# A three-engine scan put into the order of the source: a Trainium2 trunk of a gating MLP, an RWKV-7 layer and two ConvFFNs

## The chip, the core and the metric

The kernel runs on one core of one Trainium2 chip. A core has TensorE (PE, matrix products into PSUM), VectorE (DVE), ScalarE (ACT) and GpSimd (POOL), each with an instruction queue of its own, and SyncE (SP), which here only starts transfers. Each queue is a program of its own, and semaphores order the engines among each other. The metric is the device time of one execution in microseconds; lower is better. The kernel before has a median of 1274.5 us over three runs (1272.83 to 1276.07).

## The reference

One sequence of 512 positions with 1024 features goes through two residual layers. Layer 0 is a gating MLP (SGU) and a ConvFFN, layer 1 an RWKV-7 mixer and a ConvFFN; each sub-layer has an RMSNorm ahead of it. The part of the RWKV mixer that the change touches is the scan, for 16 heads of 64:

```python
def step(state, inp):
    r_t, w_t, k_t, v_t, a_t, b_t = inp
    sa = jnp.einsum('bhvk,bhk->bhv', state, a_t)
    state = (state * w_t[:, :, None, :]
             + sa[..., None] * b_t[:, :, None, :]
             + v_t[..., None] * k_t[:, :, None, :])
    y_t = jnp.einsum('bhvk,bhk->bhv', state, r_t)
    return state, y_t
```

and what follows it: a group norm of `y` per head, a bonus term, a gate `g = sigmoid(xg @ g1) @ g2` with `xg` a mix of the normalized input and its shifted copy, and the output projection `(y * g) @ w_o`.

## The kernel before, in words

**Tiling.** Activations lie transposed, as eight tiles of 128 features by 512 positions. Every dense weight product is done in three float32r products (`mm3`, lines 317 to 319: high part by high, high by low, low by high), each 128 rows by 128 columns of the array with 512 columns streamed. One such triple is a step of `dense_steps`.

**The chunked scan.** The 512 positions are cut into 8 chunks of 64 (`NCH`), and the 16 heads into two groups `g` of eight, four tiles `i` by two halves `hd` of the partitions. Within a chunk the recurrence becomes matrix products. `pairs` builds the operands of each chunk (line 935 and 949: products 64 rows deep and 128 columns wide) and sends them to DRAM; `invert(g)` inverts the 64 by 64 triangular matrices of a group. Its part for 32 by 32 blocks is a ladder on VectorE, 31 pairs of a product (line 1011) and a sum (line 1012), behind it two transposes (1017, 1018), and then 32 by 32 products on TensorE (1030, 1033) whose results ScalarE copies (1038, 1043, 1045). The group 1 ladder stands at the border of the pairs and the scan.

**One chunk of the scan** (`scan`) is this chain. Eight products `us` (line 1194, 128 rows by 64 columns) need the state `vu`; VectorE copies them to `wt` (1196). Eight products with the inverse `ti` (1207, 64 by 64) need `wt`; VectorE copies one half of their result back to `vu` (1208), ScalarE the other (1209). Eight products with `bt` (1216) need both halves; VectorE adds `s0` to them (1219, two instructions) and so writes the `vu` of the next chunk. `s0` comes from GpSimd (1203). Off this chain lie eight products `e` (1198) and eight more (1221) that make the output `y`, copied by ScalarE (1224). After each second chunk `finish` normalizes 128 positions of `y`: square on ScalarE (1237), sum on VectorE (1240), a power on GpSimd (370), a product on VectorE (1243), four transposes on TensorE (1247) and four multiply-adds on VectorE (1250).

**What fills TensorE between them.** `fill` is one long generator: the projections of `r`, `k` and `v` with their followers (`value`: transposes at 829 with copies at 834, a product of 512 columns at 844, an addition at 846, an activation at 847; line 842 makes the weights of 844), then `gates`, then the output projections (`project`). In `gates`, `gate_mix(k)` prepares one of eight operands: ScalarE scales (1054), VectorE combines (1055), ScalarE rounds to the high part (236), VectorE subtracts to get the low part (237). It cannot emit the gates of a group before all of that group's `y` is normalized.

**What sets the order.** `weave` steps the scan and puts steps of `fill` behind marked TensorE instructions at given rates. Between the remaining choices a scheduler decides: it orders each engine's queue by priority and by when it reckons an instruction to be ready. So in the scan a ready dense product may be queued ahead of a chain product that the scheduler expects later.

## Time and profile before

| | |
|---|---|
| median of three runs | 1274.5 us (1272.83 to 1276.07) |
| the profiled execution's own time | 1274.33 us |
| its span | 1272.5 us |
| TensorE matmuls busy | 1254.8 us, 7591 instructions |
| VectorE busy | 856.5 us |
| ScalarE busy | 629.6 us |
| first instruction at which the two programs' TensorE orders differ | 710.47 us |
| first product of the first chunk (line 1194) | 737.85 us |
| first product of group 1's first chunk | 803.77 us |
| end of the common stretch: from 874.22 us on TensorE's order is the same again | 874.22 us |

The trace numbers lines by the kernel before. One 32-bit product of the program shows as two matmul records, so that a set of eight shows as x16. Rows of a timeline give start and length in us; a matmul's length is modelled and overlaps its successor, so what a product costs TensorE is read from start to start. Rows of groups give the count, the busy sum in us and the mean of one in ns.

### The profile page before, as it was taken

How to read it: one execution, taken by the hardware profiler on the slowest of the kernel's cores; microseconds unless marked ns; L12 is line 12 of the kernel's file. 1: busy time of each engine (PE TensorE's matmuls, PEld its weight loads, DVE VectorE, ACT ScalarE, POOL GpSimd, SP SyncE). 2: the span in 40 equal slices, each digit the busy share in tenths (PEclk: the TensorE clock that was granted, in tenths of full speed). 3: DMA queues.
4: the chain of work that ended last, by engine and by line, in shares of the span. 5: the costliest groups of instructions: out<-in, count | busy, mean ns of one | idle time of the engine just before them, and what ended most of it. 6: DMA issues, size and time to landing. Idle time of an engine off the chain costs nothing.

```text
span 1272.5 us, 19534 instructions
## 1 busy us (share of the span) xinstructions
PE 1254.8 (99%) x7591; PEld 1014.3 (80%) x7591; DVE 856.5 (67%) x1403; ACT 629.6 (49%) x1082; POOL 98.0 (8%) x119
## 2 busy tenths in 40 slices
PE   9999999999999999999999999999999999999997
PEld 6878888888888888887777776677888888888886
DVE  6466568888886444675789887665677777772233
ACT  5534446555555333475686647423544444443232
POOL 4100200000000000000000022222100000000002
PEclk9999999999999999999999999999999999999999
DMA  7332357887556775335878698763233332233332
GB/s 251 108 99 83 123 173 239 244 255 240 198 169 209 216 231 161 105 106 182 220 203 226 202 245 206 203 181 133 83 99 100 100 99 91 94 94 106 93 91 79
DMA packets 115452, 201.65 MB, mean 158 GB/s; under 512 B 21600, under 2 KB 53600, under 8 KB 115360
## 3 DMA queue, kind: packets, MB, share of 16 engines
q10 hardware_dynamic: 39104, 112.87, 29.4%
q1 hardware_dynamic: 76256, 87.54, 23.1%
q8 instruction: 59, 0.97, 0.3%
q14 instruction: 33, 0.27, 0.1%
HBM read 152.93 MB, written 47.45 MB: 157 GB/s over the span
## 4 chain that ended last, share of the span: by engine, by line
PE 90%; DVE 4%; issue 1%; DMA 0%; POOL 0%; ACT 0%; DVEq 0%; ACTq 0%; POOLq 0%
PE mm L317 10%; PE mm L319 9%; PE mm L318 9%; PE aux L317 6%; PE aux L319 6%; PE aux L318 6%; PE e L318 6%; PE e L317 6%; PE e L319 6%; PE us L319 5%; PE us L318 5%; PE us L317 5%; PE aux L935 1%; PE aux L949 1%; PE us L1194 1%; PE e L1221 1%
## 5 line engine op out<-in xcount | busy, mean ns | idle before, releaser
L236 ACT CAST w<-w 128x512 fp32r<-128x512 f32 x340 | 206.8, 611 | 364.6 <-PE aux L319 91.8
L237 DVE TENSOR_TENSOR w<-w,w 128x512 fp32r<-128x512 f32 x340 | 232.1, 685 | 185.2 <-ACT w L236 184.7
L317 PE MATMUL mm<-mxh,w 128*128 128x512 f32 (+1 forms) x416 | 170.5, 410 | 0.0
L318 PE MATMUL mm<-mxl,w 128*128 128x512 f32 (+1 forms) x416 | 164.6, 396 | 0.0
L319 PE MATMUL mm<-mxh,w 128*128 128x512 f32 (+1 forms) x416 | 164.3, 395 | 0.0
L344 POOL TENSOR_TENSOR ss<-ss,sq 128x512 f32<-128x512 f32 x30 | 40.6, 1353 | 771.1 <-issue 592.9
L317 PEld LDWEIGHTS mm<-mxh,w 128*128 128x128 f32 (+1 forms) x416 | 77.6, 187 | 20.0 <-issue 3.3
L319 PEld LDWEIGHTS mm<-mxh,w 128*128 128x128 f32 (+1 forms) x416 | 77.8, 187 | 17.4 <-issue 0.7
L318 PEld LDWEIGHTS mm<-mxl,w 128*128 128x128 f32 (+1 forms) x416 | 77.9, 187 | 16.1 <-issue 1.3
L542 ACT ACTIVATE cv<-z,par 128x512 f32<-128x512 f32 x88 | 71.7, 817 | 28.1 <-DVE z L540 23.1
L317 PE MATMUL aux<-mxh,w 128*128 128x512 f32 x216 | 84.5, 391 | 0.0
L319 PE MATMUL aux<-mxh,w 128*128 128x512 f32 x216 | 84.2, 390 | 0.3 <-DVE w L237 0.3
L317 PE MATMUL us<-mxh,w 128*128 128x512 f32 x216 | 84.5, 391 | 0.0
L318 PE MATMUL aux<-mxl,w 128*128 128x512 f32 x216 | 84.1, 389 | 0.0
L318 PE MATMUL us<-mxl,w 128*128 128x512 f32 x216 | 84.1, 389 | 0.0
L319 PE MATMUL us<-mxh,w 128*128 128x512 f32 x216 | 84.0, 389 | 0.0
L317 PE MATMUL e<-mxh,w 128*128 128x512 f32 x208 | 81.4, 391 | 0.1
L318 PE MATMUL e<-mxl,w 128*128 128x512 f32 x208 | 81.1, 390 | 0.1
L319 PE MATMUL e<-mxh,w 128*128 128x512 f32 x208 | 80.9, 389 | 0.0
L543 DVE SCALAR_TENSOR_TENSOR cv<-z,par,cv 128x512 f32<-128x512 f32 x88 | 66.1, 752 | 20.0 <-ACT cv L542 20.0
L544 DVE SCALAR_TENSOR_TENSOR cv<-z,par,cv 128x512 f32<-128x512 f32 x88 | 66.0, 752 | 2.9
L319 PEld LDWEIGHTS aux<-mxh,w 128*128 128x128 f32 x216 | 40.5, 187 | 9.2 <-DVE w L237 0.8
(1088 smaller groups left out, 2599.0 us busy)
## 6 DMA issues: line engine op xcount, KB each, us to landing
w<-in_wup ACTq DMA_DIRECT2D x88, 512.0 KB, 3.7
w<-in_wdn ACTq DMA_DIRECT2D x32, 512.0 KB, 3.6
st<-std SPq DMA_DIRECT2D x30, 320.0 KB, 6.1
w<-wkd ACTq DMA_DIRECT2D x16, 512.0 KB, 4.8
w<-wvd ACTq DMA_DIRECT2D x16, 512.0 KB, 5.6
w<-wod ACTq DMA_DIRECT2D x16, 512.0 KB, 4.3
w<-in_wdn ACTq DMA_DIRECT2D x16, 384.0 KB, 3.3
w<-in_wsu ACTq DMA_DIRECT2D x8, 512.0 KB, 3.8
```

The source lines that it names most:

```text
L236: nc.scalar.copy(hi[r, :n], src)
L237: (lo_eng or nc.vector).tensor_tensor(lo[r, :n], src, hi[r, :n].bitcast(F32), ALU.subtract)
L317: mm(acc, wh, xh, start=first, stop=False)
L318: mm(acc, wh, xl, start=False, stop=False)
L319: mm(acc, wl, xh, start=False, stop=last)
L344: nc.gpsimd.tensor_tensor(self.ss, self.ss, self.sq, ALU.add)
L542: nc.scalar.activation(c, z[:, 2:], AF.Identity, scale=cw(2, i), bias=self.p("conv_b", l * 44 + i))
L543: nc.vector.scalar_tensor_tensor(c, z[:, 1:T + 1], cw(1, i), c, ALU.mult, ALU.add)
L544: nc.vector.scalar_tensor_tensor(c, z[:, 0:T], cw(0, i), c, ALU.mult, ALU.add)
L935: nc.tensor.matmul(qs[hd][:, c - ch.start, :], bk[H[hd], c, C * hd:C * hd + P], ar[H[hd], c, :], start=True, stop=True)
L949: nc.tensor.matmul(qs[hd][:, c, :], bk[H[hd], c, C * hd:C * hd + P], dg[H[hd], c, :], start=True, stop=True)
L1194: nc.tensor.matmul(us[H[hd], 0, i, :], ar(i, hd, 0), vu[:, hd, i, :], start=True, stop=True)
```

## The change

One function `recurrence` takes the place of the two woven scans. It walks both groups in one loop inside a block in which TensorE, VectorE and ScalarE keep the order in which the source emits instructions. Within a chunk:

- The products 1207 of a chunk stand directly behind the eight output products (1221 before, 1189 now) of the chunk ahead of it, which need the same 64 by 64 mode; the output products of a chunk are so put off by one chunk (`pend`).
- Dense work comes in two blocks, behind the products with `ti` and behind those with `bt` (`pump`), each of two steps of `fill` as long as `fill` has dense work.
- The copies of the chain (1208, 1209) are emitted first; output copies, `finish` (in `slot`s), group 1's inversion (`side`) and `fill` come behind them. `finish` goes at most one step per slot.
- `for _ in range(AHEAD)` lets eight steps of group 1's inversion be emitted for one of group 0's, ahead of the scan. The ladder's instructions stand in the program ahead of the block, and the scheduler places them.
- Weight loads of the scan stretch go by SP's queue, no longer by ScalarE's (`self.wq`).
- The gate's second weight part is padded with zeros from 32 to 128 columns, so that its products use the whole array.
- The last `value` takes a bank of `aux`, and the two first mixes and the gate weights are fetched at other steps.

Lines move: 1194, 1196, 1198, 1207, 1208, 1209, 1216, 1219, 1221, 1224 become 1242, 1244, 1246, 1257, 1258, 1259, 1268, 1271, 1189, 1193; 1011, 1012, 1017, 1018, 1030, 1038, 1043 become 1020, 1021, 1026, 1028, 1040, 1048, 1053; 317 to 319 become 325 to 327; 829, 834, 842, 844, 846, 847 become 838, 843, 851, 853, 855, 856; 236 and 237 become 240 and 241, 255 to 257 become 259 to 261; 1054 and 1055 become 1064 and 1065.

```diff
@@ -32,6 +32,9 @@
 
 RATES = ((1.9, 2), (1.9, 6, 2.2), (0.66, 2, 1.15), (0.72, 2), (2, 2), (1.2, 6, 2.2))
 LEAD = 1
+AHEAD, SUBST, PRODUCTS, PUMP = 8, 5, (0, 0, 0, 0, 0, 2, 3, 3), (1.3, 1.3)
+MID = (1.3, 1.3)
+MIDDLE, END = 1, 2
 WB = 4
 FIRST0, WAIT, STEPS = 1, 1, (2, 2, 2, 2, 2)
 NKEY = 3
...
@@ -302,7 +306,10 @@
         t = [self.wp.tile([P, 1024], F32, tag="w32", bufs=2, name=self.uid("w32")) for _ in range(2)]
         for i in range(2):
             self.wq.dma_start(t[i], self.gd[:, i, 0:1024])
-        return (1024, [tuple(x.bitcast(F32R) for x in t)]), (512, [self.pair(self.gd[:, :, 1024:], 256)])
+        w = self.pair(self.gd[:, :, 1024:], 256)
+        for x in w:
+            self.nc.gpsimd.memset(x[:, 256:384].bitcast(F32), 0.0)
+        return (1024, [tuple(x.bitcast(F32R) for x in t)]), (512, [w])
 
     @staticmethod
     def wcols(w, c, n, rows=slice(None)):
...
@@ -314,6 +321,7 @@
 
         mm = self.nc.tensor.matmul
         (wh, wl), (xh, xl) = w, x
+        self.work += 3 * (acc.shape[-1] + 32) / 2400
         mm(acc, wh, xh, start=first, stop=False)
         mm(acc, wh, xl, start=False, stop=False)
         mm(acc, wl, xh, start=False, stop=last)
...
@@ -840,7 +849,7 @@
                 yield
             wb = ip.tile([P, P], F32, tag="wb", bufs=1, name=self.uid("wb"))
             S.activation(wb, self.c("bones", P), AF.Copy, scale=self.p("r_k", m))
-            q = self.acc("mm")
+            q = self.acc("aux" if m == KT - 1 else "mm")
             nc.tensor.matmul(q, wb, rt[g][:, i, :], start=True, stop=True)
             b = rt[g][:, i, :]
             V.tensor_tensor(b, q, v, ALU.mult)
...
@@ -1163,14 +1173,56 @@
                 nc.sync.dma_start(bt, btd[c][:, ps])
             chunks[g, c] = st, bt, vu
 
-        left, two = [], []
-
-        def scan(g, late=iter(())):
-
-            ih = [(i, hd) for i in range(4) for hd in range(2)]
+        two, pend, lates = [], [], []
+
+        def heads():
+            return [(i, hd) for i in range(4) for hd in range(2)]
+
+        def outputs(copy=True):
+
+            if not pend:
+                return
+            g, c, st, vu, e, y = pend[0]
+            if copy is not None:
+                for i, hd in heads():
+                    o = RW * (1 - hd)
+                    nc.tensor.matmul(e[H[hd], 0, i, :], st[i][H[hd], o:o + C], vu[H[hd], hd, i, :],
+                                     start=False, stop=True, skip_group_check=True)
+            if copy is not False:
+                for hd in range(2):
+                    S.copy(y[H[c % 2], :, hd, :], e[H[hd], 0])
+                if c % 2 == 1:
+                    lates.append([finish(g, c // 2, y), MIDDLE])
+                pend.pop()
+
+        def slot(place):
+
+            for late in list(lates):
+                if late[1] != place:
+                    continue
+                with ExitStack() as ctx:
+                    for eng in (mybir.EngineType.PE, mybir.EngineType.DVE):
+                        ctx.enter_context(tc.issue_after(self.last(eng)))
+                    more = next(late[0], None)
+                if more is None:
+                    lates.remove(late)
+                else:
+                    late[1] = more
+
+        def pump(us):
+
+            self.owed += us
+            while self.owed > 0:
+                before = self.work
+                if next(fill, self) is self:
+                    return
+                self.owed -= max(self.work - before, 0.1)
+
+        def recurrence(side):
+
+            ih = heads()
             y = None
-
-            for c in range(NCH):
+            for g, c in itertools.product(range(2), range(NCH)):
                 last = c == NCH - 1
                 if (g, c) not in chunks:
                     load(g, c)
...
@@ -1201,33 +1249,36 @@
                     s0 = tile_([P, 4, C], "wt", 4)
                     for hd in range(2):
                         G.tensor_tensor(s0[H[hd]], vu[H[hd], hd], bc(gc[H[hd], 4 * g:4 * g + 4, c], C), ALU.mult)
-                self.step(late)
-                yield
+                if g == 1 and c == 0:
+                    for _ in side:
+                        pass
+                outputs(False)
                 for i, hd in ih:
                     nc.tensor.matmul(us[H[hd], 1, i, :], ti[g][H[hd], i, c, :], wt[H[hd], i, :], start=True, stop=True)
                 V.tensor_copy(vu[h0, 0], us[h0, 1])
                 S.copy(vu[h1, 1], us[h1, 1])
-                self.step(late)
-                if g == 1 and c == 0:
-                    self.step(late)
-                yield
+                outputs(None)
+                pend.append((g, c, st, vu, e, y))
+                slot(MIDDLE)
+                if g == 0 and c < SUBST:
+                    self.step(side)
+                pump(MID[g])
                 if not last:
                     for i, hd in ih:
                         nc.tensor.matmul(us[H[hd], 0, i, :], bt[:, i, hd, :], vu[:, hd, i, :], start=True, stop=True)
                     nvu = chunks[g, c + 1][2]
                     for hd in range(2):
                         V.tensor_tensor(nvu[H[hd], hd], us[H[hd], 0], s0[H[hd]], ALU.add)
-                for i, hd in ih:
-                    nc.tensor.matmul(e[H[hd], 0, i, :], pt(i, hd), vu[H[hd], hd, i, :],
-                                     start=False, stop=True, skip_group_check=True)
-                for hd in range(2):
-                    S.copy(y[H[c % 2], :, hd, :], e[H[hd], 0])
-                self.step(late)
-                yield
-                if c % 2 == 1:
-                    yield from late
-                    late = finish(g, c // 2, y)
-            left.append(late)
+                slot(END)
+                if g == 0:
+                    for _ in range(1 if c < SUBST else PRODUCTS[c]):
+                        self.step(side)
+                pump(PUMP[g])
+            outputs()
+            while lates:
+                pump(PUMP[g])
+                slot(MIDDLE)
+                slot(END)
 
         def finish(g, b, y):
 
...
@@ -1235,13 +1286,13 @@
             ts = slice(b * P, (b + 1) * P)
             sq = tile_([P, 2 * 4, C], "ysq", 2)
             S.activation(sq, y3, AF.Square)
-            yield
+            yield END
             ss, rs = tmp("gs", 2, 8), tmp("gr", 2, 8)
             V.tensor_reduce(ss, sq, AX.X, ALU.add)
             self.rsqrt(ep, rs, ss, 1.0 / C, GN_EPS)
-            yield
+            yield MIDDLE
             V.tensor_tensor(y3, y3, bc(rs, C), ALU.mult)
-            yield
+            yield END
             q = self.acc("aux")
             for i in range(4):
                 nc.tensor.transpose(q[:, i * P:(i + 1) * P], y[:, i].rearrange("p h f -> p (h f)"), self.c("ident", P))
...
@@ -1308,18 +1358,19 @@
         ahead = invert(1)
         for _ in inv:
             next(fill)
-            self.step(ahead, (mybir.EngineType.PE,))
+            for _ in range(AHEAD):
+                self.step(ahead, (mybir.EngineType.PE,))
         ctx.close()
         ep = ctx.enter_context(tc.tile_pool(name="scan", bufs=1))
         inv = ahead
         r.sg = [ep.tile([P, T], F32R, name=f"sg{i}") for i in range(3)]
         for _ in range(LEAD):
             next(fill, None)
-        self.weave(scan(0), inv, fill, *RATES[2], ktiles=STEPS[2])
-        for _ in inv:
-            pass
-        self.weave(scan(1, left.pop()), None, fill, *RATES[3], ktiles=STEPS[3])
-        self.weave(left.pop(), None, fill, *RATES[4], ktiles=STEPS[4])
+        self.ktiles, self.work, self.owed = 1, 0.0, 0.0
+        self.wq = nc.sync
+        with tc.manual_schedule(engines={mybir.EngineType.PE, mybir.EngineType.DVE, mybir.EngineType.Activation}):
+            recurrence(inv)
+        self.wq = nc.scalar
         for _ in fill:
             pass
         ctx.close()
```

**VectorE, from the first chunk's `wt` to the next chunk's.** Before (`tt` and `pr` are the ladder of group 1's inversion, `rb` and `vu` the state, `gwl` a gate weight):

```order
L1196 COPY wt_6667<-us_6657 128x256
L1012 TENSOR_TENSOR tt_6617<-tt_6617,pr_6618 128x11x21
L1011 TENSOR_TENSOR pr_6618<-li_6616,tt_6617 128x240
L1012 TENSOR_TENSOR tt_6617<-tt_6617,pr_6618 128x12x20
L1208 COPY rb_6438<-us_6657 64x256
L1011 TENSOR_TENSOR pr_6618<-li_6616,tt_6617 128x247
L1012 TENSOR_TENSOR tt_6617<-tt_6617,pr_6618 128x13x19
L237 TENSOR_TENSOR gwl_6997<-w_1096_6705,gwh_6996 128x512
L1011 TENSOR_TENSOR pr_6618<-li_6616,tt_6617 128x252
L1219 TENSOR_TENSOR vu_6652<-us_6657,wt_6677 64x256 x2
```

and of the change (33 ladder instructions stand between line 1258 and the first transpose, of which the first two and the last are shown):

```order
L1244 COPY wt_6745<-us_6735 128x256
L1021 TENSOR_TENSOR tt_6601<-tt_6601,pr_6602 128x14x18
L1020 TENSOR_TENSOR pr_6602<-li_6600,tt_6601 128x255
L1258 COPY rb_6418<-us_6735 64x256
L1021 TENSOR_TENSOR tt_6601<-tt_6601,pr_6602 128x15x17
L1020 TENSOR_TENSOR pr_6602<-li_6600,tt_6601 128x256
...
L1021 TENSOR_TENSOR tt_6601<-tt_6601,pr_6602 128x31
L1026 STREAM_TRANSPOSE ix_6770<-tt_6601 128x32x32
L1271 TENSOR_TENSOR vu_6730<-us_6735,wt_6755 64x256 x2
L1028 STREAM_TRANSPOSE li_6771<-tt_6601 128x32x32
L855 TENSOR_TENSOR rt_4350<-mm_6803,v_6708 128x512
L1244 COPY wt_6831<-us_6821 128x256
```

The first chunk's addition into the next state now stands behind the whole rest of the ladder and one transpose, where before three ladder instructions and a weight's low part stood between it and the copy.

**TensorE, around the start of the fourth chunk.** Before (`us` and `e` are chain and output products, `mm` dense ones):

```order
L1221 MATMUL e_6839<-vu_6742,st_6738 64x64
L829 MATMUL mm_6982<-cst,v_6903 128x128 x3
L1216 MATMUL us_6838<-vu_6742,cbt_6741 64x64 x8
L1221 MATMUL e_6839<-vu_6742,st_6738 64x64 x7
L829 MATMUL mm_6982<-cst,v_6903 128x128
L317 MATMUL mm_6905<-mxh_5515,w_1070_6509 128x512
L1194 MATMUL us_6945<-vu_6742,st_6834 64x64
L1198 MATMUL e_6946<-vu_6742,st_6834 64x64
L318 MATMUL mm_6905<-mxl_5516,w_1070_6509 128x512
L1194 MATMUL us_6945<-vu_6742,st_6834 64x64 x7
L1198 MATMUL e_6946<-vu_6742,st_6834 64x64 x7
L1247 MATMUL aux_6968<-cst,y_6656 128x128 x4
```

and the third chunk of the change (`aux` is a product of group 1's inversion):

```order
L1242 MATMUL us_6948<-vu_6817,st_6813 64x64 x8
L1246 MATMUL e_6949<-vu_6817,st_6813 64x64 x8
L1189 MATMUL e_6822<-vu_6730,st_6726 64x64 x8
L1257 MATMUL us_6948<-wt_6958,ti_4860 64x64 x8
L1040 MATMUL aux_6995<-ix_6770,ti_4861 32x32 x16
L325 MATMUL mm_6918<-mxh_5515,w_1086_6711 128x512
L326 MATMUL mm_6918<-mxl_5516,w_1086_6711 128x512
L327 MATMUL mm_6918<-mxh_5515,w_1086_6711 128x512
L853 MATMUL mm_7026<-rt_4350,wb_7024 128x512
...
L1268 MATMUL us_6948<-vu_6817,cbt_6816 64x64 x8
```

Sets of eight are no longer cut in two with dense products between, and sets of one mode stand together. From the first chunk's first product to the last chunk's end, TensorE's order holds 63 runs of full-array products before and 28 now, and 81 runs of sets 64 columns wide before and 46 now.

**ScalarE, from the second chunk's state copy to the third's.** Before:

```order
L1209 COPY vu_6652<-us_6746 64x256
L236 CAST mxh_7009<-sq_7006 128x512
L1224 COPY y_6656<-e_6747 64x4x64 x2
L1237 ACTIVATE ysq_6861<-y_6656 128x512
L842 ACTIVATE wb_7103<-cst,par 128x128
L847 ACTIVATE rt_4350<-rt_4350,par 128x512
L818 COPY v_6903<-mm_6700 128x512
L247 DMA w_1232_7771<-wod_136 128x2x512
L1209 COPY vu_6742<-us_6838 64x256
```

and of the change:

```order
L1259 COPY vu_6730<-us_6821 64x256
L1193 COPY y_6734<-e_6736 64x4x64 x2
L1048 COPY ti_4861<-li_6771 32x32x32 x2
L827 COPY v_6916<-mm_6710 128x512
L843 COPY vt_6922<-mm_6923 64x4x64 x4
L259 CAST gw_6933<-w_1088_6715 32x512
L260 CAST gw_6933<-w_1088_6715 32x512
L240 CAST gwh_6937<-w_1088_6715 128x512
L1259 COPY vu_6817<-us_6948 64x256
```

Two copies of the inversion, four of `vt` and three of the gate's weights now stand between two state copies. VectorE subtracts the gate's low parts (261, 241) ahead of that third chunk's `wt` copy (1244), and its next rows are:

```order
L1258 COPY vu_6817<-us_6948 64x256
L855 TENSOR_TENSOR rt_4350<-mm_7026,v_6916 128x512
L1065 SCALAR_TENSOR_TENSOR sq_7030<-h_66,omu,sq_7030 128x512
L241 TENSOR_TENSOR mxl_7034<-sq_7030,mxh_7033 128x512
L1271 TENSOR_TENSOR vu_6817<-us_6948,wt_6968 64x256 x2
```

so that one `gate_mix`, with its ScalarE instruction between 1065 and 241, stands ahead of the addition that starts the next chunk.

## The prediction

> **What bounds the kernel now.** I read the page first, then the busy time by stretches around the scan, then TensorE's timeline, VectorE's, and last the groups by line between 560 and 1000 us.

> ```profile
> PE 1254.8 (99%) x7591; PEld 1014.3 (80%) x7591; DVE 856.5 (67%) x1403; ACT 629.6 (49%) x1082; POOL 98.0 (8%) x119
> ...
> st<-std SPq DMA_DIRECT2D x30, 320.0 KB, 6.1
> ```

> ```profile
> 710.00:720.00 10.00, 9.47 (x137) 6.83 (x136) 7.12 (x12) 5.07 (x9) 1.12 (x2) 1.00 0.60 167
> ...
> 727.00:734.00 7.00, 7.00 (x95) 5.57 (x89) 6.31 (x19) 3.68 (x9) 1.04 (x2) 0.52 0.43 119
> ...
> 740.00:800.00 60.00, 57.98 (x922) 42.34 (x921) 48.18 (x105) 35.80 (x69) 16.21 (x19) 1.00 0.89 220
> 800.00:862.00 62.00, 59.63 (x783) 43.14 (x781) 40.94 (x93) 21.41 (x47) 14.91 (x16) 1.00 0.69 188
> 862.00:874.00 12.00, 11.09 (x62) 9.17 (x57) 5.89 (x15) 2.15 (x5) 1.63 (x1) 1.00 0.52 173
> ```

> TensorE is the bound nearly everywhere. The columns of the stretches are length, busy time of TensorE, of its weight loads, of VectorE, ScalarE and GpSimd, then granted clock and DMA. From 710.47 us, where the two orders part, to 874.22, where they meet again, are 163.75 us. In them TensorE idles only 0.53 + 2.02 + 2.37 + 0.91 = 5.8 us. One stretch runs at a clock of 0.52. But VectorE is busy 48 of 60 us in the first half of the scan and ScalarE 36: two engines with little room stand beside the bound one.

> TensorE's timeline shows what its own order costs:

> ```profile
> 745.74 0.50 PE L317 MATMUL mm<-mxh,w 128*128 128x512 f32 x1
> 746.08 0.39 PE L318 MATMUL mm<-mxl,w 128*128 128x512 f32 x1
> 746.31 0.40 PE L319 MATMUL mm<-mxh,w 128*128 128x512 f32 x1
> ...
> 747.33 0.68 PE L1207 MATMUL us<-wt,ti 64*64 64x64 f32 x16
> 747.95 0.50 PE L317 MATMUL mm<-mxh,w 128*128 128x512 f32 x1
> ...
> 751.81 0.69 PE L1194 MATMUL us<-vu,st 128*64 128x64 f32 x16
> 752.33 0.64 PE L1198 MATMUL e<-vu,st 128*64 128x64 f32 x16
> 752.89 0.50 PE L317 MATMUL mm<-mxh,w 128*128 128x512 f32 x1
> ```

> ```profile
> 730.14 0.77 PE L317 MATMUL mm<-mxh,w 128*128 128x512 f32 x1
> 730.71 0.63 PE L318 MATMUL mm<-mxl,w 128*128 128x512 f32 x1
> ```

> Start to start, a dense product costs 0.23 us (746.08 to 746.31). The run of six from 745.74 to 747.33 takes 1.59, so a change of mode on both sides adds 0.21 to a run. A set of sixteen alone costs 0.62 (747.33 to 747.95), two of one mode together 1.08 (751.81 to 752.89), so an end of a narrow run costs 0.16; a set cut in two costs somewhat more, and I take 0.20.

> **What the change saves.** The counts shown with the change's order are 63 runs of dense products before and 28 after, 81 narrow runs before and 46 after: 35 x (0.21 + 0.20) = 14.4 us of TensorE. The slow stretch from 727 to 734 did work that costs about 3.8 us at full clock (0.43 us and more a product there, from 730.14, instead of 0.23): 3.0 us, which need not come back. TensorE's own work is therefore 163.75 - 5.8 - 3.0 = 154.9 before and 140.5 after. If it waited as little as before, the change would gain 14 to 17 us. The zero columns cost nothing on TensorE, since a product streams its 512 columns whatever the width of its weights, and their two fills go to GpSimd, busy 8%. The loads moved past to SP's queue have cover while a chunk takes over 6.1 us, the landing of `st`; uncovered, each would cost up to that once. The other edits (the bank of the last `value`, the steps at which gate weights and mixes are fetched, eight inversion steps for one) add no instruction; their effect is the place of their instructions in the queues, counted below.

> **What it costs: waits.** The three queues now keep the source's order, and each link of the chain has other work ahead of it. The bare links:

> ```profile
> 803.77 0.69 PE L1194 MATMUL us<-vu,st 128*64 128x64 f32 x16
> ...
> 804.51 0.42 DVE L1196 COPY wt<-us 128x256 f32<-128x256 f32 x1 [1.66 <-PE us L1194]
> ...
> 805.29 0.68 PE L1207 MATMUL us<-wt,ti 64*64 64x64 f32 x16
> ...
> 806.07 0.42 DVE L1208 COPY vu<-us 64x256 f32<-64x256 f32 x1 [1.14 <-PE us L1207]
> ```

> ```profile
> 821.28 0.42 DVE L1208 COPY vu<-us 64x256 f32<-64x256 f32 x1 [1.11 <-PE us L1207]
> ...
> 821.78 0.37 ACT L1209 COPY vu<-us 64x256 f32<-64x256 f32 x1 [2.16 <-DVE vu L1208]
> ...
> 822.25 0.69 PE L1216 MATMUL us<-vu,cbt 128*64 128x64 f32 x16
> ...
> 823.05 0.87 DVE L1219 TENSOR_TENSOR vu<-us,wt 64x256 f32<-64x256 f32 x2
> ```

> 0.74 + 0.42 to `wt`; 0.78 to VectorE's half of the state, ScalarE's half 0.50 later and 0.37 long; 0.80 + 0.44 to the first half of the next state. With 0.05 for each hand-over to TensorE that is 4.2 us a chunk, under the 6 to 7 us that TensorE's sets and dense blocks take. So some 2.5 us of foreign work a chunk is free, and what is more becomes waiting. These are the rows of the foreign work:

> ```profile
> 711.67 2.01 DVE L1017 STREAM_TRANSPOSE ix<-tt 128x1024 f32<-128x1024 f32 x1
> ...
> 728.00 0.19 DVE L1011 TENSOR_TENSOR pr<-li,tt 128x31 f32<-128x31 f32 x1
> 728.22 0.19 DVE L1012 TENSOR_TENSOR tt<-tt,pr 128x31 f32<-128x31 f32 x1
> ```

> ```profile
> L1012 DVE TENSOR_TENSOR tt<-tt,pr 128x31 f32<-128x31 f32 (+15 forms) x62 | 22.3, 360 | 1.4
> L1011 DVE TENSOR_TENSOR pr<-li,tt 128x31 f32<-128x31 f32 (+15 forms) x62 | 21.6, 349 | 1.4
> L834 ACT COPY vt<-mm 64x256 f32<-64x256 f32 x32 | 11.7, 366 | 9.4 <-PE mm L829 7.3 <-issue 1.7
> L1224 ACT COPY y<-e 64x256 f32<-64x256 f32 x32 | 11.7, 366 | 17.8 <-PE e L1221 17.5
> L1038 ACT COPY ti<-li 32x1024 f32<-32x1024 f32 x8 | 8.3, 1043 | 6.1 <-DVE li L1018 4.8 <-DVE rs L369 1.1
> L1054 ACT ACTIVATE sq<-h,par 128x512 f32<-128x512 f32 x8 | 5.8, 724 | 1.9 <-PE mm L319 1.7
> L1055 DVE SCALAR_TENSOR_TENSOR sq<-h,omu,sq 128x512 f32<-128x512 f32 x8 | 6.0, 745 | 1.2 <-ACT sq L1054 1.2
> L846 DVE TENSOR_TENSOR rt<-mm,v 128x512 f32<-128x512 f32 x8 | 5.5, 687 | 2.7 <-PE mm L844 2.7
> L236 ACT CAST mxh<-sq 128x512 fp32r<-128x512 f32 x8 | 4.9, 616 | 3.4 <-DVE sq L1055 3.3
> L1043 ACT COPY tt<-aux 32x512 f32<-32x512 f32 x8 | 4.6, 577 | 1.0 <-PE aux L1030 0.9
> L842 ACT ACTIVATE wb<-cst,par 128x128 f32<-128x128 f32 x7 | 2.8, 404 | 1.9 <-PE mm L844 1.9
> ```

> *First chunk, the ladder.* One ladder is half of 22.3 + 21.6, with 0.03 between instructions (728.00 + 0.19 to 728.22): 23.9 us. It starts near 728.0 as before, since it hangs on ScalarE's copies. Ahead of the addition into the second chunk's state stand all of it, line 846 (0.69), the two copies (0.42 each) and one transpose (2.0): 728.0 + 23.9 + 3.5 = 755.4, and 755.9 with the first addition. TensorE's first chunk starts near 737.5, for a PSUM bank of its last dense block comes free only with line 846, behind ten pairs. Its own work up to the second chunk's first product is 1.1 + 0.6 + 2.3 + 0.6 + 2.4 and 0.7 of waiting for `wt`, so it stands from 745.2 to 755.9. I take 10.3, and 11.4 with the smaller waits of this chunk. Behind the addition come the other transpose and another 846 ahead of the next `wt`: 2.0 + 0.7 + 0.4 against 1.6 us of sets: 1.4, with the rest 1.8.

> *Third chunk, ScalarE.* Behind the four transposes of line 829 come four copies (4 x 0.37), three casts (0.62 each), a subtraction (0.69) and `wt` (0.42), 4.6 us with hand-overs, against 2.4 of TensorE work: 2.2. Then the weights of line 844 stand on ScalarE behind two `y` copies, a square (0.63), two copies of 1043, one of 1038 and 842 itself, 4.0 us behind the state copy, which ends 1.65 after its set began; TensorE fills 2.0: 3.7. Then 844, 846, 847, and one mix with its round trip: 0.86 + 0.69 + 0.72 + 0.72 + 0.75 + 0.62 + 0.69 + 0.42 and seven hand-overs, 5.8, against 4.5: 1.2, with 0.4 for the second half. Sum 7.5.

> *Elsewhere.* Each of the eight mixes blocks VectorE for 0.75 + 0.62 + 0.69 and two hand-overs, 2.2 us, where before its four parts lay among others. The same walk down the queues gives, in us: 4.2 ahead of the first chunk; fourth chunk 2.9; fifth 4.9, of which 4.2 are the weights of 844 again (842 behind the state copy's 1.65, two `y` copies 0.74, square 0.63, two inversion copies 1.16, and a whole mix with its round trip 2.2, then 0.40, in all 6.8 against 2.6 of TensorE work); sixth 1.5; seventh 4.7; group 1 with its first chunk, whose `wt` stands behind the activated gate's three round trips (3.7) and where `fill` has no dense work until `y` of group 0 is normalized, 16.1 to the end. All waits: 4.2 + 11.4 + 1.8 + 7.5 + 2.9 + 4.9 + 1.5 + 4.7 + 16.1 = 55.0.

> **Unknown sizes.** The hand-overs: 0.02 or 0.09 instead of 0.05 moves the walk by -2 to +7. The clock: a fall like that at 727 costs 3.0 us in full work, less where TensorE would wait anyway; from 0 to five falls, 0 to 10 us. I take one, behind the ten-microsecond stand, at 2.0, since before there was one.

> [...]

> **Sum.** 140.5 + 55.0 + 2.0 = 197.5 us against 163.75: +33.8. On the profiled execution's 1274.33 us (span 1272.5 and 1.8 around it, within 0.2 of the median) that is 1308 us.

> **Rivals.** *Faster: only the ladder binds.* If the dense blocks cover every round trip, the waits are 4.2 + 11.4 + 1.8: 140.5 + 17.4 + 2.0 = 159.9, 3.9 less: 1270, and 1265 when half of those 4.2 and the 1.8 and the clock's 2.0 vanish too. It decides at about 2.5 us of foreign work per chunk; for it speaks that ScalarE has 24 of 60 us free, against it that the freedom is spread while the queues' order is not. *More falls of the clock.* Five in all give +8: 1316 to 1330. [...] *Half the waits.* If the later waits absorb one another, as a wait on one link gives the next engine time to catch up, 37 us of them become 18: 1289. Against it: I walked them in order, so each already starts from the last.

> **How the numbers follow.** Forecast 0.62 (1295 to 1321); more falls 0.13; half the waits 0.14; only the ladder 0.11. A difference under 0.3% (3.8 us) cannot be told from none. Slower by more 0.88, within 0.02, faster 0.10. The range 1285 to 1327 leaves out the faster case, the low end of the halved one and the high end of the falls.

> **What would show it.** Right: TensorE stands some 10 us ahead of the second chunk's first product (line 1242) with VectorE in line 1020 and 1021; 3 to 4 us ahead of 853 in the third and fifth chunk, released by ScalarE; group 0 takes 90 to 95 us from its first chunk to group 1's, against 66 now; dense runs of six at 1.59. Wrong: a second chunk that starts before 750, or chunks of 6 to 7 us in group 0.

## The result, and the profile after

The changed kernel has a median of 1311.6 us over four runs (1309.0 to 1314.4), the kernel before 1273.7 (1271.5 to 1276.1): a ratio of 1.0298, with a 95% interval of 1.0269 to 1.0327. It is slower by 38 us. The forecast was 1308 in a range of 1285 to 1327. The profiled execution took 1311.7 us with a span of 1309.9. One run of a kernel below, the one with no engine in order, took 3121.6 us where the other nine took 1279 to 1288; it is left out of the numbers.

The page of the change, busy times and then the granted clock in 40 slices:

```profile
PE 1249.7 (95%) x7591; PEld 1015.0 (77%) x7591; DVE 855.4 (65%) x1403; ACT 629.4 (48%) x1082; POOL 98.3 (8%) x121
...
PEclk9999999999999999999999988799999999999999
```

The instructions and the busy times are nearly those of before; the span is 37 us longer. All of it lies in the stretch in which the orders differ: TensorE's orders are equal up to 710.2 us and again from 911.6, 201.4 us against 163.75, a difference of 37.6 us where the spans differ by 37.4. Busy times by stretches of the change, cut near the starts of its chunks (length, TensorE, its weight loads, VectorE, ScalarE, GpSimd, granted clock, DMA):

```profile
710.00:738.00 28.00, 24.99 (x387) 18.53 (x387) 22.18 (x44) 16.34 (x29) 2.50 (x4) 0.94 0.68 174
738.00:756.00 18.00, 7.60 (x86) 5.54 (x84) 16.64 (x44) 2.13 (x6) 0.90 (x3) 0.80 0.80 174
756.00:766.00 10.00, 9.81 (x164) 7.86 (x166) 4.20 (x6) 5.03 (x9) 1.91 (x4) 0.85 0.25 69
766.00:782.00 16.00, 10.08 (x158) 6.89 (x158) 4.54 (x8) 9.85 (x18) 0.00 (x0) 0.89 0.66 160
782.00:795.00 13.00, 9.05 (x168) 7.25 (x168) 6.21 (x15) 6.40 (x14) 4.62 (x5) 1.00 0.61 172
795.00:811.00 16.00, 11.66 (x164) 7.94 (x164) 7.02 (x13) 7.13 (x14) 1.52 (x1) 0.79 0.46 114
811.00:833.00 22.00, 17.46 (x262) 13.51 (x260) 12.21 (x25) 9.33 (x19) 7.07 (x10) 1.00 0.70 183
833.00:862.00 29.00, 19.87 (x268) 16.14 (x266) 15.09 (x33) 10.02 (x22) 4.10 (x5) 0.76 0.70 164
862.00:892.00 30.00, 26.69 (x415) 21.16 (x415) 17.36 (x43) 7.64 (x18) 10.25 (x10) 1.00 0.64 165
892.00:912.00 20.00, 17.77 (x130) 14.09 (x129) 12.31 (x31) 4.09 (x10) 3.27 (x2) 1.00 0.30 98
```

In the first chunk VectorE works 16.6 of 18 us and TensorE 7.6. From 766 to 811 no engine is near its limit: TensorE, VectorE and ScalarE wait for each other in turn. That is what a chain in fixed order looks like. The biggest stands of TensorE, in its timeline (in brackets the idle time ahead of a row, counted from the modelled end of the row before it, and who released it):

```profile
755.42 1.47 PE L1242 MATMUL us<-vu,st 128*64 128x64 f32 x15 [9.75 <-DVE vu L1271]
...
770.00 0.68 PE L1257 MATMUL us<-wt,ti 64*64 64x64 f32 x16 [2.33 <-DVE wt L1244]
...
775.78 1.77 PE L853 MATMUL mm<-rt,wb 128*128 128x512 f32 x2 [3.58 <-ACT wb L851]
...
804.36 2.07 PE L853 MATMUL aux<-rt,wb 128*128 128x512 f32 x2 [3.86 <-ACT wb L851]
...
838.25 1.12 PE L1257 MATMUL us<-wt,ti 64*64 64x64 f32 x16 [3.38 <-DVE wt L1244]
```

These are the five places that the forecast named. VectorE's timeline shows what stands ahead of the first:

```profile
752.97 0.21 DVE L1021 TENSOR_TENSOR tt<-tt,pr 128x31 f32<-128x31 f32 x1
753.21 1.91 DVE L1026 STREAM_TRANSPOSE ix<-tt 128x1024 f32<-128x1024 f32 x1
754.97 0.85 DVE L1271 TENSOR_TENSOR vu<-us,wt 64x256 f32<-64x256 f32 x2
755.86 2.05 DVE L1028 STREAM_TRANSPOSE li<-tt 128x1024 f32<-128x1024 f32 x1
```

The last ladder instruction, a transpose, and only then the 0.85 us on which the next chunk hangs. And ScalarE's timeline in the third chunk, between the casts of the gate's weights and the weights of line 853:

```profile
768.15 0.62 ACT L240 CAST gwh<-w 128x512 fp32r<-128x512 f32 x1
771.31 0.37 ACT L1259 COPY vu<-us 64x256 f32<-64x256 f32 x1 [2.54 <-DVE vu L1258]
771.69 0.74 ACT L1193 COPY y<-e 64x256 f32<-64x256 f32 x2
772.46 0.63 ACT L1288 ACTIVATE ysq<-y 128x512 f32<-128x512 f32 x1
773.10 1.16 ACT L1053 COPY tt<-aux 32x512 f32<-32x512 f32 x2
774.28 1.04 ACT L1048 COPY ti<-li 32x1024 f32<-32x1024 f32 x1
775.33 0.40 ACT L851 ACTIVATE wb<-cst,par 128x128 f32<-128x128 f32 x1
```

ScalarE is idle for 2.5 us, since its next instruction is a state copy that is not ready; the weights (851), which read only constants, stand behind it and six further instructions. In a fixed order an engine can be idle and late at once.

### The profile page after: what moved, and what is told of

The parts are those of the page before. It is cut to its first block, busy times and chain, and to the rows that moved or that the text cites. A ratio compares the mean times of both kernels' runs of the same rounds, so it can differ in the third digit from the quotient of the medians.

```text
span 1309.9 us, 19542 instructions
## 1 busy us (share of the span) xinstructions
PE 1249.7 (95%) x7591; PEld 1015.0 (77%) x7591; DVE 855.4 (65%) x1403; ACT 629.4 (48%) x1082; POOL 98.3 (8%) x121
## 5 line engine op out<-in xcount | busy, mean ns | idle before, releaser
L325 PE MATMUL mm<-mxh,w 128*128 128x512 f32 x416 | 172.9, 416 | 2.5 <-DVE rt L855 1.5
L327 PE MATMUL mm<-mxh,w 128*128 128x512 f32 x416 | 164.1, 395 | 0.0
L326 PE MATMUL mm<-mxl,w 128*128 128x512 f32 x416 | 163.9, 394 | 0.0
L325 PEld LDWEIGHTS mm<-mxh,w 128*128 128x128 f32 x416 | 78.8, 189 | 24.4 <-issue 4.4
L327 PEld LDWEIGHTS mm<-mxh,w 128*128 128x128 f32 x416 | 78.7, 189 | 17.3 <-issue 0.7
L326 PEld LDWEIGHTS mm<-mxl,w 128*128 128x128 f32 x416 | 78.8, 189 | 16.3 <-issue 2.5
L550 ACT ACTIVATE cv<-z,par 128x512 f32<-128x512 f32 x88 | 71.7, 817 | 28.9 <-DVE z L548 23.9
```

What stands on the lines that cost most here:

```text
L325: mm(acc, wh, xh, start=first, stop=False)
L326: mm(acc, wh, xl, start=False, stop=False)
L327: mm(acc, wl, xh, start=False, stop=last)
L550: nc.scalar.activation(c, z[:, 2:], AF.Identity, scale=cw(2, i), bias=self.p("conv_b", l * 44 + i))
```

## The experiments

Each ratio is to the kernel before, run beside it on the same chip, with its 95% interval. The edits start from the changed kernel where nothing else is said.

**Which engine's order costs what.** Four kernels take engines out of the block that keeps the source order:

```diff
-        with tc.manual_schedule(engines={mybir.EngineType.PE, mybir.EngineType.DVE, mybir.EngineType.Activation}):
+        if True:                                                                      # no_order
+        with tc.manual_schedule(engines={mybir.EngineType.PE}):                       # order_pe
+        with tc.manual_schedule(engines={mybir.EngineType.PE, mybir.EngineType.DVE}): # order_pe_dve
+        with tc.manual_schedule(engines={mybir.EngineType.PE, mybir.EngineType.Activation}): # order_pe_act
```

> The change with the source order given up on all three engines; the scheduler orders their queues again, and everything else of the change stays (outputs put off, loads on SP's queue, ladder ahead, zero columns). TensorE's order then holds 48 dense and 71 narrow runs in the scan instead of 28 and 46 (63 and 81 before): 20 x 0.21 + 25 x 0.20 = 9.2 us of the saved 14.4 are gone. Theory (the source order of the queues exposes ladder and round trips): some 47 us of TensorE standing become 12 to 20: 1311.6 + 9 - 31 = 1290 at the most, likelier 1275 to 1285, and no stand of over 5 us ahead of line 1242. Rival (loads, put-off outputs or the ladder ahead do it, not the order): 1300 to 1320. Rival (the clock alone): 1311.6 less the 12 or so us that five falls can cost at most, 1300.

> Source order on TensorE alone, VectorE and ScalarE free for the scheduler. TensorE's order is that of the change, mode by mode. Theory: TensorE keeps the 14.4 us saved by fewer mode changes and loses most waits that come from foreign work ahead of a chain copy (ladder 11.4 and 1.8, ScalarE ahead of 853 in the third and fifth chunk 7.9, casts 2.2, about 4 more): 1311.6 - 27 = 1285, range 1278 to 1294. Rival (TensorE's own order is what waits): 1305 to 1315. Rival (free queues hide everything): 140.5 us of own work and 6 of waiting, 17 below before, 1257.

> Source order on TensorE and VectorE, ScalarE free. Theory: what hangs on ScalarE's order goes (853 in the third and fifth chunk 3.6 and 3.9 by the trace, the casts 2.3, some second-half state copies 3.6): 1311.6 - 13 = 1298, range 1293 to 1303, and the 10 us ahead of the second chunk's first product stay. If VectorE's order alone carries the loss: 1308 to 1314. If ScalarE's alone does: as with TensorE alone, near 1285.

> Source order on TensorE and ScalarE, VectorE free. Theory: the stand ahead of the second chunk's first product (9.8 us) goes or becomes smaller, the waits on ScalarE ahead of 853 stay: 1311.6 - 15 = 1296, range 1290 to 1303. If ScalarE's order alone carries the loss: 1308 to 1314. If VectorE's alone does: near 1285.

| source order on | median, us | ratio to before |
|---|---|---|
| no engine | 1282.5 | 1.0060 (1.0037 to 1.0083) |
| TensorE | 1283.2 | 1.0065 (1.0043 to 1.0087) |
| TensorE, VectorE | 1297.3 | 1.0165 (1.0123 to 1.0207) |
| TensorE, ScalarE | 1297.7 | 1.0179 (1.0140 to 1.0219) |
| all three (the change) | 1311.6 | 1.0298 (1.0269 to 1.0327) |

VectorE's order adds 1.00% (12.7 us) to TensorE's, ScalarE's 1.14% (14.5 us), both together 2.33% (29.7 us). The sum of the two apart is 27.2 us, which the intervals do not tell from 29.7, and neither engine alone carries the loss.

The loss has two parts in the profiled executions. From 710.2 us to where the orders are the same again, TensorE idles 29.7 us with itself alone in order, 36.0 with VectorE, 34.3 with ScalarE and 47.0 with all three. Of its busy time there, 9.5, 23.7, 35.6 and 26.6 us are at half clock. There dense products follow each other in 0.43 us instead of 0.23, so about half of that time is lost; by this estimate VectorE's order adds 6 us of idle time and 7 of slower work, ScalarE's 5 and 13.

TensorE's waits by line and releaser (total, times, longest), first with the order on TensorE alone, then with VectorE, then with ScalarE:

```profile
PE aux L1040 <- DVE ix L1026: 12.0, 2, 10.5
PE us L1268 <- ACT vu L1259: 8.1, 8, 1.7
```

```profile
PE us L1242 <- DVE vu L1271: 13.4, 4, 9.7
PE us L1257 <- DVE wt L1244: 12.2, 8, 4.0
```

```profile
PE aux L1040 <- DVE ix L1026: 10.7, 2, 9.2
...
PE mm L853 <- ACT wb L851: 4.7, 1, 4.7
PE aux L853 <- ACT wb L851: 3.9, 1, 3.9
```

With VectorE in order the ten microseconds stand ahead of the next chunk (1242), as in the change, and the waits on 851 are gone. With ScalarE in order it is the other way round. But with VectorE free the ten microseconds do not go: they stand ahead of line 1040, a product of group 1's inversion that needs the ladder's end and has a fixed place in TensorE's second chunk. So the ladder stops TensorE through TensorE's own order too, where my account of the change had put this down to VectorE's alone. With no engine in order the waits on 1040, 851 and `wt` are small, and one of another kind is the longest:

```profile
PE us L1242 <- DMA st<-std: 5.2, 1, 5.2
PE us L1268 <- ACT vu L1259: 2.6, 2, 1.8
```

That kernel keeps 48 dense runs and 71 narrow ones on TensorE, and so, by the estimate from the forecast's rows, 5.2 us of the 14.4.

**The ladder in one lump or spread.** Four ladder steps instead of eight ahead of the scan; the rest is emitted within the chunks:

```diff
-AHEAD, SUBST, PRODUCTS, PUMP = 8, 5, (0, 0, 0, 0, 0, 2, 3, 3), (1.3, 1.3)
+AHEAD, SUBST, PRODUCTS, PUMP = 4, 5, (0, 0, 0, 0, 0, 2, 3, 3), (1.3, 1.3)
```

> The change in full, with four ladder steps instead of eight emitted for each step of group 0's inversion ahead of the scan. The rest of the ladder is then emitted in the scan, behind the sets, a step per half chunk, instead of standing in one lump ahead of the addition into the second chunk's state. Theory (a lump counts because a chunk has only some 2.5 us of slack): the 9.8 us ahead of the second chunk's first product go; two pairs (1.5 us) in each half of the following chunks take some of their slack, which the mixes and casts there also want, and give some back: -12, 1300, range 1295 to 1306. Rival (all work ahead of the chain counts, wherever it stands): 1308 to 1314. Rival (the chunks' slack takes it all): 1311.6 - 14.8 of waits ahead of 1242 = 1297 and no longer later chunks.

Measured 1300.3 us, ratio 1.0203 (1.0179 to 1.0226). The first chunk falls from 17.8 to 8.0 us and the second from 10.5 to 7.2; the sixth to eighth grow from 7.2, 10.2 and 4.9 to 10.0, 14.1 and 6.6. The forecast gain came (11.3 us, 12 forecast), net of what was given back: the same work costs less spread out than in a lump.

**The mixes' round trips.** The last six of eight mixes are left out:

```diff
         def gate_mix(k):
+            if k >= 2:
+                return gx[0]
             with ExitStack() as behind:
```

> The change in full without the last six of the eight mixes: their four instructions are left out and the gate's products take the first mix's operand in their place, so that the gate is another one; TensorE does the same products. Theory: each mix blocks VectorE's queue for 2.2 us (0.75 + 0.62 + 0.69 and hand-overs), and ScalarE's behind it, ahead of a chain copy: 6 x 2.2 = 13.2, and up to 24 if the waits of both halves of a chunk shrink with it: 1288 to 1299. Rival (mixes hide in the slack, only ladder and lines 851 and 259 count): 1306 to 1312.

Measured 1300.6 us, ratio 1.0205 (1.0179 to 1.0232): 11 us, just outside the range I gave (12.6 at least). The fifth chunk falls from 15.5 to 12.7 us and the seventh from 10.2 to 6.0; the third and fourth, where casts of the gate's weights and line 853 bind, do not fall. So a mix costs about 1.8 us here, less than the 2.2 that it holds VectorE.

**The clock.** The granted clock was at half five times in the stretch: 3.4 us from 714.7, 10.2 from 748.8, 3.4 from 776.1, 6.8 from 803.4 and 13.7 from 837.6, 37.5 us in all, where the forecast had one fall. To price them, useless dense products fill four stands (`du` is a bank that nothing reads then):

```diff
+                if (g, c) == (0, 1):
+                    for _ in range(10):
+                        nc.tensor.matmul(us.rearrange("p a i f -> p (a i f)"), self.c("bones", P), rt[1][:, 0, :], start=True, stop=True)
...
+            for _ in range(4 if m >= KT - 2 else 0):
+                nc.tensor.matmul(q, self.c("bones", P), rt[g][:, i, :], start=True, stop=True)
             nc.tensor.matmul(q, wb, rt[g][:, i, :], start=True, stop=True)
...
+                for _ in range(7 if (g, c) == (1, 0) else 0):
+                    nc.tensor.matmul(du[:, 256:512], self.c("bones", P), rt[1][:, 0, 0:256], start=True, stop=True)
```

> The change in full with dense products without a use put into four stands of TensorE: ten (two records of 0.43 us each) ahead of the second chunk's first product, four ahead of 853 in the third and fifth chunk, seven of half the width ahead of 1257 in group 1's first chunk. Their results are overwritten or not read. It takes the idle away and leaves the waits. Falls of the clock in the change's trace: 748.8 to 759.1, 776.1 to 779.5, 803.4 to 810.3, 837.6 to 851.2, of which TensorE works some 3.7, 3.4, 5.9 and 8 us at half speed: 10 us of price at the most. Theory (the queues' waits set the time, and a slower TensorE is mostly absorbed in them): 0 to 5 less, 1307 to 1312. Rival (the clock is a main cost): 10 less, 1302 or under. If idle time is what brings the falls, at least the first three of these are gone; if the clock falls for another reason they stay. If the useless products are longer than the stands, up to 1314.

Measured 1310.6 us, ratio 1.0285 (1.0256 to 1.0314), no difference from the change. The falls of the second and the fifth chunk are gone and group 1's lasts only 3.4 us, but the third chunk's lasts 6.8 us, and two of 3.4 us are new (from 794.3 and 825.0). Half clock is down to 20.5 us. Between 710 and 912 us, the change and this kernel:

```profile
710.00:912.00 202.00, 155.00 (x2179) 118.92 (x2178) 117.75 (x255) 77.95 (x154) 36.13 (x42) 0.91 0.61 154
```

```profile
710.00:912.00 202.00, 171.19 (x2230) 126.07 (x2229) 117.87 (x257) 78.59 (x155) 36.61 (x42) 0.95 0.59 154
```

TensorE is busy 171.2 us, of which the useless products are 21.0 (8.7 + 5.3 + 3.7 + 3.3), so 150.2 for its own work against 155.0 in the change. These 4.8 us came back as waits: the second chunk takes 10.5 us as before, and its set 1257 now waits 1.4 us for `wt`, where in the change slower sets had filled that time. The test is not perfect, since in the third chunk the useless products ran at half clock and lasted longer than the stand (18.3 us instead of 16.3), and group 1 was 2 us shorter. So a gain of some 3 us from a full clock is possible, but not the 10 of the rival.

**Why the order on TensorE alone did not win.** With it, and four ladder steps ahead:

```diff
-AHEAD, SUBST, PRODUCTS, PUMP = 8, 5, (0, 0, 0, 0, 0, 2, 3, 3), (1.3, 1.3)
+AHEAD, SUBST, PRODUCTS, PUMP = 4, 5, (0, 0, 0, 0, 0, 2, 3, 3), (1.3, 1.3)
...
-        with tc.manual_schedule(engines={mybir.EngineType.PE, mybir.EngineType.DVE, mybir.EngineType.Activation}):
+        with tc.manual_schedule(engines={mybir.EngineType.PE}):
```

> Source order on TensorE alone, and four ladder steps instead of eight ahead of the scan, so that the inversion's first 32 by 32 products stand later in TensorE's order. With eight, TensorE stood 10.5 us ahead of line 1040 (VectorE's ladder and transposes not done). Theory: that stand goes, 1283.2 - 10 = 1273, range 1268 to 1278, level with the kernel before or a little faster. Rival (the ladder is late wherever the product stands): 1280 to 1285.

Measured 1277.7 us, ratio 1.0025 (1.0011 to 1.0040). The stand ahead of 1040 is gone, and a new one takes part of its place. TensorE's waits, and then the transfers on SP's queue (a row's length is issue time, with waiting in it):

```profile
PE us L1242 <- DMA st<-std: 6.1, 1, 6.1
```

```profile
798.07 1.20 SPq L251 DMA_DIRECT2D w<-wod  x2
799.32 4.47 SPq L1157 DMA_DIRECT2D st<-std  x4
803.89 6.75 SPq L1163 DMA_DIRECT2D vu<-vtd  x2
```

The state operands of group 1's second chunk stand on SP behind the weights that the change moved there; the product that needs them starts at 811.8. So the loads go back to ScalarE's queue:

```diff
-        self.wq = nc.sync
```

> Source order on TensorE alone and four ladder steps ahead, as in the run before it, and the weight loads of the scan stretch back on ScalarE's queue. With them on SP's queue TensorE stood 6.1 us ahead of line 1242 for st<-std in group 1's second chunk, its four transfers issued on SP behind 512 KB of w<-wod and 320 KB of the gate's weights. Theory (the move to SP's queue costs up to one landing once the chunks are short): the stand goes, 1277.7 - 6 = 1272, range 1269 to 1275. Rival (the transfers themselves are late, 16 engines are busy there whichever queue starts them): 1276 to 1279. Rival (a load's issue now stands ahead of a state copy in ScalarE's queue): 1279 to 1283.

Measured 1273.7 us, ratio 0.9988 (0.9971 to 1.0005): 0.37% less than with the loads on SP, and level with the kernel before. Between 710 and 875 us, the kernel before and this one:

```profile
710.00:875.00 165.00, 159.17 (x2182) 118.15 (x2181) 118.80 (x258) 78.55 (x156) 35.13 (x40) 0.98 0.74 193
```

```profile
710.00:875.00 165.00, 145.31 (x2177) 114.00 (x2176) 116.26 (x257) 78.54 (x156) 34.99 (x42) 0.96 0.72 186
```

TensorE does the same work in 13.9 us less, at a clock that is a little lower. The forecast had 14.4 us for fewer mode changes, and this order has as few dense and narrow runs as the change; no run alters the mode changes alone. All of it now stands as idle time, since TensorE idles 19.7 us instead of 5.8.

**Dense work kept for group 1.** On top of that, single steps in the last three chunks of group 0:

```diff
-                pump(MID[g])
+                pump(MID[g] if g or c < 5 else 0.68)
...
-                pump(PUMP[g])
+                pump(PUMP[g] if g or c < 5 else 0.68)
```

> The same with dense blocks of one step instead of two in the last three chunks of group 0, so that group 1's first chunk has 12 dense products where it had none (7 in the kernel before). Group 1's first chunks had no dense work, TensorE stood 1.0 to 1.4 us ahead of 1268 in each, and the clock was at half for 13.7 us there. Theory: the dense products do the covering: 1.4 + 1.0 of stands and 3 to 4 us of clock less, some waits in the shorter chunks of group 0 given back: 3 under the run with the loads back, 1267 to 1271, faster than the kernel before. Rival (the shorter chunks of group 0 wait for VectorE instead): level, 1271 to 1275.

Measured 1273.2 us, ratio 0.9991 (0.9978 to 1.0005): level, as the rival had it. The long fall of the clock that I meant to avoid was already gone with the 6.1 us stand. GpSimd's timeline of this kernel shows what holds up the state copies in three chunks instead:

```profile
827.07 1.94 POOL L378 TENSOR_TENSOR gr<-rs,mhalf 128x8 f32<-128x8 f32 x1 [11.16 <-DVE rs L377]
828.97 2.15 POOL L1251 TENSOR_TENSOR wt<-vu,gc 64x256 f32<-64x256 f32 x2
```

The product `s0` (1251) reads the state at the chunk's start. That was written by 824.7 us, yet GpSimd sits idle until the power of `finish` (378), queued ahead of it, has its input. The state copies overwrite what `s0` reads, and so wait: ScalarE's 1259 7.4 us in three places, with TensorE behind them.

**The power behind `s0`**, first in the change itself, with all three engines in order:

```diff
-MIDDLE, END = 1, 2
+MIDDLE, END, EARLY = 1, 2, 3
...
                         G.tensor_tensor(s0[H[hd]], vu[H[hd], hd], bc(gc[H[hd], 4 * g:4 * g + 4, c], C), ALU.mult)
+                slot(EARLY)
...
             V.tensor_reduce(ss, sq, AX.X, ALU.add)
+            yield EARLY
             self.rsqrt(ep, rs, ss, 1.0 / C, GN_EPS)
```

> The change in full, with one edit: finish emits its power (VectorE's small product and GpSimd's 378) behind the two GpSimd products s0 (1251) of the next chunk and no longer ahead of them. In the change's trace GpSimd waits for VectorE ahead of 378 while s0 could run (863.96: 2.06 us behind 13.5 idle, and 1251 only then), and ScalarE's state copy 1259 waits 15.0 us in three places for 1251, VectorE's 1258 3.1. Theory (an engine busy 8% is in the chain here): 1.6 to 2 us in each of four or five chunks less, 1311.6 - 8 = 1304, range 1301 to 1307. Rival (VectorE and ScalarE are late there anyway): 1309 to 1314.

Measured 1310.3 us, ratio 1.0278 (1.0257 to 1.0298): my theory fell. ScalarE's 15.0 us of waiting for `s0` became 0 (3.6 us for the power in its place), and group 1 from its first chunk to its last is 54.6 us instead of 57.8, but group 0 97.8 instead of 95.5, with half clock for 44.4 us of the stretch instead of 37.5. The waits did shrink: from 710.2 us to where the orders are the same again, TensorE idles 42.7 us instead of 47.0. But its busy time grows as much, from 154.4 to 158.8 us, with 33.8 us of it at half clock instead of 26.6. And in the change most of ScalarE's wait lay beside other waits of TensorE: only 3.6 us of TensorE's stands were for 1259. I had priced the idle time of an engine for which TensorE mostly did not wait.

Then where the chunks are short, with five ladder steps ahead instead of four:

```diff
-AHEAD, SUBST, PRODUCTS, PUMP = 4, 5, (0, 0, 0, 0, 0, 2, 3, 3), (1.3, 1.3)
+AHEAD, SUBST, PRODUCTS, PUMP = 5, 5, (0, 0, 0, 0, 0, 2, 3, 3), (1.3, 1.3)
```

> Source order on TensorE alone, loads on ScalarE's queue, single dense steps in the last three chunks of group 0, now with the power behind s0 and five ladder steps ahead instead of four. In the run with the dense products kept GpSimd's s0 stood behind the power in six chunks (827.07 power, 828.97 s0, ScalarE's state copy waits 3.9, TensorE 1.3); VectorE and ScalarE waited 12 us there, TensorE 7.3 for 1259. Theory: 3 to 4 of TensorE's stands go, 2 to 3 more with the inversion a step earlier: 1273.2 - 6 = 1267, range 1263 to 1270, faster than the kernel before by about 0.5%. Rival (the stands move to the next link): 1271 to 1274, no difference.

Measured 1268.8 us, ratio 0.9955 (0.9941 to 0.9970): faster than both kernels, by 0.45% than the one before. Its page:

```profile
PE 1238.5 (98%) x7591; PEld 1007.6 (79%) x7591; DVE 854.2 (67%) x1403; ACT 628.7 (50%) x1082; POOL 98.0 (8%) x121
```

Group 1, from its first chunk to its last, takes 48.3 us instead of 53.9 in the kernel without the last edit, group 0 65.6 instead of 64.6, and the first chunk starts 2.1 us later. Ladder steps belong to group 0's stretch, so the gain is most likely the power's; the two edits were not run apart.

## Why the prediction was right, step by step

- **The sum.** Forecast 197.5 us for the stretch, measured 201.4; 1308 against 1311.6. By term, from the change's trace: TensorE is busy 154.4 us in the stretch, 26.6 of them at half clock, so its own work at full clock is 141.1 (140.5 forecast) and the clock's price 13.3 (2.0 forecast); the waits are 47.0 (55.0 forecast). The clock's error of 11.3 and the waits' of 8.0 nearly cancel. That the sum came within 3.9 us is in part luck.
- **The saving.** 14.4 us of TensorE work, estimated by counting mode changes: 13.9 less busy time in the kernel with the loads back. The 0.20 for a set cut in two was my estimate; in the trace before, the two parts of a set of line 1221, at 807.25 and 809.43, cost 0.26 + 0.61 = 0.87 us from start to start, 0.25 more than a whole set's 0.62. That the zero columns cost nothing is in that trace too: products on 32 columns of the array follow each other there in 0.23 to 0.24 us (802.37, 802.61, 802.84), as those on 128 do.
- **The waits.** Forecast by place, from start to start, against idle time in the stretches above, from modelled ends: ahead of the first chunk 4.2, measured 3.0; first 11.4, 10.4; second 1.8, 0.2; third 7.5, 5.9; fourth 2.9, 4.0; fifth 4.9, 4.3; sixth to eighth 6.2, 4.5; group 1 16.1, 14.7. Together 55.0 against 47.0. Part of the 8 us is the tail of a matmul ahead of each wait, which idle time does not count (a dense product's row lasts 0.40 us where the next starts 0.23 behind it). The single stands came out at 9.75 (10.3 forecast), 3.58 (3.7), 2.33 (2.2), 3.86 (4.2) and 3.38 (3.7). The signs held too: the second chunk started at 755.4 (755.9), group 0 took 95.5 us (90 to 95). Of the signs of being wrong, chunks of 6 to 7 us in group 0, only the eighth chunk came near one, with 4.9 us.
- **The clock: mis-sized.** The step took one fall at 2.0 us; there were five. That its one fall would stand behind the ten-microsecond wait, and that the rival had five, were assumptions of mine, which the trace of before does not show: ahead of the one fall there, from 727.3 us, TensorE is busy without a break from 713.8 on. In the change one began within that wait, at 748.8, and four elsewhere. The five cost TensorE 13.3 us by the estimate above. The rival with five falls had the count right and the time wrong (1316 to 1330), since it added their price to all 55.0 us of waits. In the run with useless products 17 us less of half clock gained nothing beyond the noise, and the 4.8 us of faster work came back as waits; with the power behind `s0` 4.3 us of waits came back as slower work. So the two terms trade against each other. Together they were 60.3 us, 57.0 forecast.
- **Half the waits, and the ladder alone: wrong.** The waits came to 47.0 us, not to the 36 of the rival, and VectorE's and ScalarE's orders cost 29.7 us together, no less than the 27.2 of both apart. With the ladder spread the ratio was still 1.0203.
- **Where the cause was put too narrowly.** The ladder's ten microseconds were argued as VectorE's queue. They are also TensorE's: with VectorE free the same ladder stops TensorE at 1040.
- **The loads on SP.** I had said that they have cover while a chunk takes over 6.1 us and cost up to one landing without it. In the change no stand of TensorE is due to them; in shorter chunks one is, of 6.1.
- **Left out.** GpSimd's order has no term in the sum. In the change that was harmless, as the run on it showed; where the chunks are short it is probably worth some 5 us (group 1's 48.3 us against 53.9).

## What to carry to other kernels

Fixing the order of one engine saves what that engine pays for a bad order; fixing the order of the engines that it waits for makes every independent instruction in their queues a possible wait of the first. Count, for each link of the recurrence, what stands ahead of it in each queue, and compare with the cover that the bound engine has there, lump by lump, for a lump costs more than the same work spread (11.3 us more here). When such a wait is removed, look next at the engines and queues that had slack only because the loop was long: here the load queue, then GpSimd.

## What the runs showed of the hardware

By the forecast's rows six dense products between narrow sets took 1.59 us, 0.21 more than six at 0.23, and two narrow sets of one mode 1.08 where one alone took 0.62, so 0.16 for an end of a narrow run. With 35 runs fewer of each kind TensorE is busy 13.9 us less between 710 and 875 us, in the kernel with the loads back (145.3 against 159.2, at a clock of 0.96 against 0.98). How much of that the mode changes are was not shown by a run of its own.

```profile
767.33 0.68 PE L1191 MATMUL e<-vu,st 64*64 64x64 f32 x16
770.36 1.12 PE L1266 MATMUL us<-wt,ti 64*64 64x64 f32 x16 [2.35 <-DVE wt L1250]
```

```profile
766.00:770.40 4.40, 2.06 (x52) 1.60 (x50) 1.80 (x3) 3.03 (x7) 0.00 (x0) 1.00 0.82 230
770.40:777.20 6.80, 6.80 (x55) 4.32 (x56) 0.42 (x1) 4.33 (x8) 0.00 (x0) 0.50 0.75 183
```

The clock fell behind an idle time of 2.35 us, where in the change the same set stands 2.33 us, up to 770.0, and the clock stays full until 776.1. So the length of that idle time does not tell the two apart, and no run here shows what does. In group 1 of the change the clock stayed at half while TensorE worked on sets of 64 columns between 838.3 and 848.5 us, and was full from 851.2 on; the first dense products there start at 849.3.
